# A two-layer hybrid backbone: the input projection by seven products instead of eight, and its outputs through DRAM

## The chip, the cores and the metric

The kernel runs on one core of one Trainium2 chip. A core has TensorE (PE in the profile) for matmuls, VectorE (DVE), ScalarE (ACT) and GpSimd (POOL) for elementwise work, and SyncE (SP), which here only starts transfers. Each engine works through its own instructions in their order and waits for the others by semaphores. Times are microseconds of one execution on the device; the time of a kernel is the median of its runs.

## The reference, cut to what matters

Two layers over 1024 tokens of a sample and 128 tokens of a prompt, width 1024. The prompt is computed with the same weights, without the cached keys. For each layer:

```
hn   = rms_norm(x, g_pre) * (1 + scale) + shift        # scale, shift, gate from w_mod
proj = hn @ w_in                                       # 1024 x 7456
a_b, a_c, a_x, a_z, q_down, kv_down, b_z, c_u, c_z, merge_logits = split(proj)
y_a  = silu(a_z) * (a_b * conv3(a_c * a_x))
y_b  = silu(b_z) * attention(rms_norm(q_down) @ w_uq, [cache, rms_norm(kv_down) ...] @ w_ukv)
y_c  = silu(c_z) * (pool(c_u) @ pool_w) * pool_scale   # window means of 2, 4, 8, 16 tokens
merged = sum(sigmoid(merge_logits) * (y_n @ w_branch[n]) for n in a, b, c)
x    = x + gate * rms_norm(merged @ w_o, g_post)
```

## The kernel before, in words

All large products are float32 products made of three: each operand is split in a high part that TensorE's float32r format holds, and a low part with the rest. `mm3` (line 107) issues high x high, high x low and low x high by `mm` (line 105), each 128x128 weights against up to 512 columns. A split takes a cast (`a_copy`, ACT, or `p_copy`, POOL) for the high part and a subtraction on DVE (`sub`, line 88) for the low one.

The sample's tokens are held with features on the partitions, in two chunks of 512 tokens. `hn` of a chunk is 8 contraction blocks, split (`hn_tile`). w_in comes in 15 groups of 512 columns (the last 256), in weight tiles of 128x1024 that SP loads, POOL or ACT casts and DVE completes (`pump`). There are 44 slots of 128x1040 (`S`), 12 of 128x512 (`H`) and 8 accumulators of 128x512 (`PS`). `in_group` (line 471) multiplies a group: four blocks of 128 columns for chunk 0 (`prod_m`), the prompt with its tokens on the partitions (`prod_p`, 24 matmuls of 512 columns), then chunk 1 (`prod_k`).

A layer is: `conv_phase` (groups 0 to 3, the convolution after each), `merge_phase` of branch 0 (groups 4 and 5 are its gates, w_branch follows each), `pool_phase` (groups 6 to 8), `merge_phase` of branch 2 (groups 9, 10), `kvq_phase` (groups 11 to 14: latents, queries, gates of the attention branch), `produce` (queries, keys, values), `attention`, `last_merge` and `out_phase` (w_o and the norms after it). What follows an output of w_in (convolution, window sums, norms, the prompt's parts) reads it from the accumulator or from SBUF and is written out in the stretches in which the next groups are multiplied: work is kept in generators, and each `tick()` between two blocks moves the oldest ones on by one step (`spawn`, `tick`, `finish`, lines 115 to 135). So the order in each engine's queue is that in which this code calls; there is no scheduler. Only the merge's sums (`d_part`), the attention's gates and silu(b_z) go through DRAM.

In `merge_phase` an old sum is fetched one block ahead, and a store follows the product:

```
def out(c, m, gate, ps, g=g):
    mul(gate, ps, gate)
    if not first:
        add(gate, gate, old.pop((c, m)), eng=pool)
    sp.dma_start(out=d_part[4 * g + m, c], in_=gate)
```

## Time and profile before

| | |
|---|---|
| median of 3 runs | 2762.57 us (2761.93 to 2763.33) |
| span of the profiled execution | 2761.7 us, first to last instruction; 0.9 us under the median |
| PE busy | 2670.2 us (97%), 11696 matmuls recorded |
| DVE busy | 1262.9 us (46%) |
| ACT busy | 871.4 us (32%) |
| POOL busy | 677.7 us (25%) |
| mean granted clock of PE | 0.990 |
| read from HBM, written | 167.16 MB, 43.81 MB |

Busy time is the time in which an engine works on an instruction; an engine that waits in an instruction is idle. The mean of a matmul's duration (395 ns) is longer than the distance from one to the next, since they are pipelined; their rate is read from a stretch with a count. A group of instructions says how long its engine was idle right before them, and whom it waited for. The chain of waits follows the last instruction back to what released it, step by step.

### The profile page before, as it was taken

The numbers are of one execution on the slowest core, as the hardware profiler recorded it, in microseconds if no ns is written. First come the engines' busy times: TensorE is split into PE (matmuls) and PEld (weight loads), VectorE is DVE, ScalarE is ACT, GpSimd is POOL, SyncE is SP. The second block draws the span as 40 slices with busy tenths as digits, with TensorE's granted clock in tenths as the row PEclk, the third lists the DMA queues.
The fourth block names the chain that finished last, engine by engine and source line by source line (L and its number), as shares of the span: only waits on it lengthen the run. The fifth ranks groups of instructions, "written<-read, shape, count | busy, mean of one in ns | idle before, by whom it ended". The sixth has DMA issues, their size and how long they took to land.

```text
span 2761.7 us, 29939 instructions
## 1 busy us (share of the span) xinstructions
PE 2670.2 (97%) x11696; PEld 2114.9 (77%) x11696; DVE 1262.9 (46%) x1802; ACT 871.4 (32%) x1547; POOL 677.7 (25%) x598
## 2 busy tenths in 40 slices
PE   6999999999999999999989999999999999999998
PEld 3787777788888777777768888888888787777786
DVE  5532212521243378886475321134113416888655
ACT  3211111221123367773332111122102324777622
POOL 3200000001210355662132000100121023576502
PEclk8999999999999999999999999999999999999999
DMA  6111433223312100006231102202232120000333
GB/s 262 46 38 54 165 121 115 80 84 107 117 45 102 58 5 9 24 31 206 80 118 46 46 23 73 100 23 85 95 103 85 54 95 20 5 8 31 122 119 115
DMA packets 83149, 215.08 MB, mean 78 GB/s; under 512 B 10304, under 2 KB 12608, under 8 KB 83008
## 3 DMA queue, kind: packets, MB, share of 16 engines
q1 hardware_dynamic: 74656, 199.01, 21.1%
q10 hardware_dynamic: 8352, 14.16, 1.4%
q8 instruction: 92, 1.51, 0.2%
q14 instruction: 49, 0.40, 0.0%
HBM read 167.16 MB, written 43.81 MB: 76 GB/s over the span
## 4 chain that ended last, share of the span: by engine, by line
PE 85%; DVE 7%; issue 3%; ACT 3%; POOL 1%; DMA 0%; SPq 0%; DVEq 0%; ACTq 0%; POOLq 0%
PE p L105 85%; DVE s L86 4%; DVE c L1163 1%; ACT s L77 1%; ACT h L77 1%; ACT s L66 1%; POOL s L101 1%; DVE h L86 0%; DVE c L1170 0%; POOL s L86 0%; DVE s L98 0%; DMA s<-in_xT_dram 0%; DVE h L98 0%; DVE h L101 0%; ACT h L1081 0%
## 5 line engine op out<-in xcount | busy, mean ns | idle before, releaser
L105 PE MATMUL p<-s,s 128*128 128x512 f32 (+3 forms) x10948 | 2582.7, 395 | 35.0 <-DVE c L1163 13.0
L105 PEld LDWEIGHTS p<-s,s 128*128 128x128 f32 (+1 forms) x10948 | 2030.5, 188 | 551.4 <-issue 30.9
L77 ACT ACTIVATE h<-p 128x512 f32<-128x512 f32 (+1 forms) x496 | 288.3, 584 | 744.6 <-PE p L105 727.3
L86 DVE TENSOR_TENSOR s<-s,s 128x1024 fp32r<-128x1024 f32 (+5 forms) x263 | 303.2, 1163 | 422.5 <-ACT s L66 206.5
L80 POOL TENSOR_SCALAR s<-s 128x1024 fp32r<-128x1024 f32 (+2 forms) x144 | 172.5, 1201 | 1303.3 <-PE p L105 598.2
L86 DVE TENSOR_TENSOR s<-h,s 128x512 fp32r<-128x512 f32 (+3 forms) x348 | 316.7, 921 | 159.6 <-ACT s L66 90.6
L86 DVE TENSOR_TENSOR h<-p,h 128x512 f32<-128x512 f32 (+4 forms) x166 | 100.0, 609 | 317.2 <-PE p L105 278.0
L77 ACT ACTIVATE s<-p 128x512 fp32r<-128x512 f32 (+1 forms) x320 | 193.9, 606 | 105.4 <-PE p L105 101.1
L66 ACT CAST s<-s 128x1024 fp32r<-128x1024 f32 (+3 forms) x96 | 96.5, 1007 | 220.3 <-DVE s L86 122.5
L86 POOL TENSOR_TENSOR h<-h,h 128x512 f32<-128x512 f32 (+2 forms) x76 | 91.3, 1201 | 276.2 <-DVE h L86 240.7
L1163 DVE TENSOR_REDUCE c<-p 128x1 f32<-128x448 f32 x256 | 147.8, 611 | 4.3 <-PE p L105 4.1
L66 ACT CAST s<-h 128x512 fp32r<-128x512 f32 (+4 forms) x124 | 66.8, 542 | 249.5 <-DVE h L86 95.8
L86 DVE TENSOR_TENSOR h<-h,h 128x512 f32<-128x512 f32 (+8 forms) x118 | 73.9, 627 | 154.9 <-ACT h L77 149.7
L86 POOL TENSOR_TENSOR s<-s,s 64x1024 fp32r<-64x1024 f32 (+3 forms) x43 | 102.9, 2393 | 81.3 <-DVE s L86 55.2
L66 ACT COPY s<-p 64x512 f32<-64x512 f32 (+3 forms) x136 | 76.5, 568 | 129.5 <-PE p L105 125.5
L86 POOL TENSOR_TENSOR s<-h,s 128x512 fp32r<-128x512 f32 x64 | 89.2, 1393 | 113.3 <-ACT s L77 110.8
L66 ACT COPY h<-p 128x512 f32<-128x512 f32 (+3 forms) x74 | 34.1, 464 | 254.2 <-PE p L105 157.6
L86 POOL TENSOR_TENSOR s<-s,h 128x512 f32<-128x512 f32 x38 | 57.1, 1513 | 151.2 <-DVE h L98 106.7
L86 DVE TENSOR_TENSOR s<-p,s 128x512 fp32r<-128x512 f32 (+2 forms) x62 | 36.2, 586 | 93.1 <-PE p L105 75.9
L86 POOL TENSOR_TENSOR h<-h,s 128x512 f32<-128x512 f32 x32 | 51.9, 1624 | 9.0 <-DMA h<-d_bz 7.7
L77 ACT ACTIVATE h<-h 128x512 f32<-128x512 f32 (+1 forms) x50 | 31.4, 628 | 44.7 <-DVE h L101 34.7
L86 DVE TENSOR_TENSOR c<-p,vec 128x4 f32<-128x4 f32 x24 | 3.8, 157 | 87.2 <-PE p L105 87.1
(115 smaller groups left out, 845.4 us busy)
## 6 DMA issues: line engine op xcount, KB each, us to landing
s<-in_w_in_dram SPq DMA_DIRECT2D x116, 512.0 KB
s<-in_w_mod_dram SPq DMA_DIRECT2D x48, 512.0 KB
d_part<-h SPq DMA_DIRECT2D x64, 256.0 KB
h<-d_part SPq DMA_DIRECT2D x64, 256.0 KB
s<-in_w_br_dram SPq DMA_DIRECT2D x24, 512.0 KB
s<-in_xT_dram SPq DMA_DIRECT2D x16, 512.0 KB
d_gate<-h ACTq DMA_DIRECT2D x32, 256.0 KB
s<-in_w_o_dram SPq DMA_DIRECT2D x16, 512.0 KB
```

The costliest lines, as they stand in the source:

```text
L66: act.copy(out=out, in_=in_)
L77: act.activation(out=out, in_=in_, func=func, scale=scale, bias=bias)
L80: pool.tensor_scalar(out=out, in0=in_, scalar1=1.0, scalar2=0.0, op0=ALU.mult, op1=ALU.add)
L86: eng.tensor_tensor(out=out, in0=in0, in1=in1, op=op)
L101: (eng or dve).tensor_scalar(out=out, in0=in0, scalar1=s1, scalar2=s2, op0=op0, op1=op1)
L105: pe.matmul(out=out, lhsT=lhsT, rhs=rhs, start=start, stop=stop)
L1163: dve.reduce_max(out=mv[:, i, qt:qt + 1], in_=ps[:, 0:448], axis=AX.X)
```

## The change

The products of hn with w_in for the two chunks are computed by Strassen's scheme in the form with seven products. The contraction is cut in two halves, the tokens in two chunks and the columns in two blocks of 128, so a unit (`Pair`) is 256 columns of w_in; a layer has 29. Of hn there are seven sets, each of four contraction blocks and 512 tokens, split in two: 11, 21 and 22 (halves of hn itself) and T1 to T4 (sums of them, from `t_gen`); they hold 28 of the 44 slots. Of the weights there are the two halves and two sums. Six pairs of each layer are done in two steps (`early`: the two products that chunk 0 alone needs, and the prompt; later the other five). The prompt's products are now pieces of 256 columns.

All 29 pairs come first (`in_phase`). Their outputs (gates after the sigmoid, a_c * a_x, a_b * silu(a_z), c_u, silu(c_z), latents and so on) are stored in DRAM. The convolution of the sample runs from DRAM to DRAM beside the later pairs (`conv_gen`). Then `mid_phase` loads the convolution's results and runs the two merges with the pooling, the prompt's convolution and pooling, the norms of latents and queries as generators beside them; `produce` and the rest follow as before. The pieces of w_mod in the background are now fetched one at a time, one tick ahead (`mod_bg`).

The diff, cut to its core:

```diff
     def mod_bg(todo):
         for l, j in todo:
-            for i in range(2):
-                sts = [S(), S()]
-                for n, st in enumerate(sts):
-                    sp.dma_start(out=st[:, 0:1024], in_=I["w_mod"][l, j, 2 * i + n])
-                yield
+            for i in range(4):
+                st = S()
+                sp.dma_start(out=st[:, 0:1024], in_=I["w_mod"][l, j, i])
                 yield
...
+    def hn_f32(l, c, kp, x, r, on_pool=False):
...
+        for j in range(2):
+            k, o = 2 * kp + j, slice(512 * j, 512 * j + 512)
+            stt(x[:, o], x[:, o], A_(l, 1, k), r, ALU.mult, ALU.mult)
...
+    def t_gen():
+        def put(name, j, x):
+            hi, lo = S(F32R), S(F32R)
+            a_copy(hi[:, n], x[:, n])
+            sub(lo[:, n], x[:, n], f(hi[:, n]))
+            X[name][j] = (hi, lo)
...
+        for j in range(2):
+            sub(t1[j][:, n], b12[j][:, n], b11[j][:, n])
+            sub(t2[j][:, n], b22[j][:, n], t1[j][:, n])
+        for j in range(2):
+            sub(b21[j][:, n], b21[j][:, n], t2[j][:, n], eng=pool)
+        for j in range(2):
+            put("T2", j, t2[j])
+        yield
...
+    class Pair:
+        def prep(self):
+            raw = [S(), S()]
...
+                for t in range(2):
+                    src = I["w_in"][self.l, g, 2 * i + t].rearrange("p (k c)->p k c", k=2)
+                    sp.dma_start(out=raw[i][:, 512 * t:512 * t + 512].rearrange("p (k c)->p k c", k=2),
+                                 in_=src[:, :, 256 * h:256 * h + 256])
+            yield
...
+                s = [S(), S()]
+                add(part(s[0], 0), part(raw[0], 1), part(raw[1], 1), eng=pool)
+                sub(part(s[0], 1), part(raw[0], 0), part(raw[0], 1), eng=pool)
+                yield
+                sub(part(s[1], 0), part(s[0], 0), part(raw[0], 0))
+                sub(part(s[1], 1), part(raw[1], 0), part(s[1], 0))
+                yield
...
+        def prod(self, w, half, name):
+            ps = PS()
+            for i in range(4):
+                o, q = 256 * i + 128 * half, slice(512 * (i % 2), 512 * (i % 2) + 512)
+                hi, lo = X[name][i // 2]
+                mm3(ps, (w[0][:, o:o + 128], w[1][:, o:o + 128]), (hi[:, q], lo[:, q]), i == 0, i == 3)
+            return ps
...
+    def early(l, units, epis, mid, pend):
+        for b in range(0, NE, 3):
+            us = units[b:b + 3]
+            for u in us:
+                ready(u)
...
+            for u in us:
+                h = H()
+                a_copy(h, u.prod(u.w[0], 0, "11"))
...
+            for u, h in zip(us, p1):
+                v = H()
+                add(v, u.prod(u.w[1], 0, "21"), h)
...
+            finish(*pend)
+            for u in us:
+                epis[u.p][1](u.prompt())
...
+    def run(l, u, epi):
+        ready(u)
+        full = u.kind == "full"
+        p = H()
+        if full:
+            a_copy(p, u.prod(u.w[0], 0, "11"))
+            ahead(u, 1)
+            v = H()
+            add(v, u.prod(u.w[1], 0, "21"), p)
+            epi[0](0, 0, v)
+            ahead(u, 1)
+            epi[1](u.prompt())
+        else:
+            sp.dma_start(out=p, in_=d_p1[u.p])
+        ahead(u, 1)
         tick()
...
+        add(p, u.prod(u.s[1], 0, "T2"), p)
+        ahead(u, 1)
+        p5 = u.prod(u.s[0], 0, "T1")
+        v = H()
+        add(v, p5, p)
...
+    def merge(l, n, y, yp, first, pend):
...
+            nxt = fetch(0, 0)
             for m in range(4):
+                cur = nxt
+                nxt = fetch(0, m + 1) if m < 3 else fetch(1, 0)
+                out(0, m, prod_m(B, m, y_get(y), 0), cur)
                 tick()
...
+    def s_pool(l, gis, yc):
+        for gi in gis:
+            u, z = S(), S()
...
+            for c in range(2):
+                sp.dma_start(out=u[:, 8 + 512 * c:520 + 512 * c], in_=d_u[gi, c])
+                sp.dma_start(out=z[:, 512 * c:512 * c + 512], in_=d_z[gi, c])
+            yield
+            o = pooled(u, gi, 1024, [S(), S()])
...
+    def mid_phase(l):
+        yp = S(F32R)
+        gc = spawn(p_conv(l, yp))
+        ya = load_ya(l)
+        lead[0] = 4
+        fill()
+        yc, ypc = {}, S(F32R)
+        gp = [spawn(p_pool(l, ypc)), spawn(s_pool(l, range(4), yc))]
+        merge(l, 0, ya, yp, True, (gc,))
+        finish(*gp)
+        rel()
+        R = kvq_post(l)
+        for g in R["gens"]:
+            spawn(g)
         lead[0] = 5
+        merge(l, 2, yc, ypc, False, ())
         finish(*R["gens"])
...
         for l in range(L):
-            ya, yp, gens = conv_phase(l, pend, None if l else mid())
-            if l == 0:
-                spawn(gmod)
-            merge_phase(l, 0, 4, ya, yp, gens, True)
-            yc, yp, gens = pool_phase(l)
-            merge_phase(l, 2, 9, yc, yp, gens, False)
-            R = kvq_phase(l)
+            in_phase(l, units, None if l else mid(), pend)
+            R = mid_phase(l)
             A = produce(l, R)
```

The first place where the order is told is DVE's queue at the window sums of the pooling in layer 0. In the listings, a name is a buffer with its numbers (s a slot, h a half, p an accumulator), an `x2` at a row's end a count. Before, the window sums of two groups of c_u (`s382`, `s384`, in SBUF since their eviction) follow the rows of a w_mod piece, beside the next group of w_in:

```order
L86 TENSOR_TENSOR h438_2999<-p435_2991,h438_2999 128x512
L86 TENSOR_TENSOR h438_2999<-h438_2999,h439_3000 128x512
L86 TENSOR_TENSOR s442_3010<-s382_2593 128x1039
L98 SCALAR_TENSOR_TENSOR s443_3011<-s442_3010,s382_2593 128x1024
L86 TENSOR_TENSOR s443_3011<-s442_3010,invc_83 128x1
L86 TENSOR_TENSOR s443_3011<-s443_3011,s382_2593 128x1
L86 TENSOR_TENSOR s445_3017<-s443_3011,s444_3016 128x1024
L86 TENSOR_TENSOR s446_3020<-s384_2597 128x1039
L86 TENSOR_TENSOR s447_3021<-s446_3020 128x1037
```

In the changed kernel the first group (`s989`, loaded from `d_u`) stands behind the prompt's pooling (`h1003` to `h1006`), and behind it come the evictions of the first merge (`p1012`, `p1014`) and the low part of pool_w (`s1018`):

```order
L88 TENSOR_TENSOR h1004_5810<-h1004_5810,h1003_5809 128x1
L88 TENSOR_TENSOR h1006_5819<-h1004_5810,h1006_5819 128x128
L88 TENSOR_TENSOR s1007_5835<-s989_5734 128x1039
L100 SCALAR_TENSOR_TENSOR s1008_5836<-s1007_5835,s989_5734 128x1024
L88 TENSOR_TENSOR s1008_5836<-s1007_5835,invc_93 128x1
L88 TENSOR_TENSOR s1008_5836<-s1008_5836,s989_5734 128x1
L88 TENSOR_TENSOR s1010_5842<-s1008_5836,s1009_5841 128x1024
L88 TENSOR_TENSOR h991_5742<-p1012_5847,h991_5742 128x512
L88 TENSOR_TENSOR h1011_5845<-p1014_5864,h1011_5845 128x512
L88 TENSOR_TENSOR s1018_5883<-s980_5704,s1017_5882 128x512
```

The window sums moved from the stretch of a w_in group to that of the first merge's products, with the low part of the weight that the next small products read behind them.

The second place is DVE's queue in the first microseconds of layer 0 with all of x. Before, the norm of the second chunk (`s27` to `s30`) gave high and low parts at once, beside evictions and weights of the first two groups:

```order
L98 SCALAR_TENSOR_TENSOR s27_149<-s27_149,cols0_1_88,h101_469 128x512 x2
L98 SCALAR_TENSOR_TENSOR s104_491<-s27_149,cols0_1_88,s103_490 128x512 x2
L86 TENSOR_TENSOR s106_499<-s28_150,s105_498 128x512 x2
L86 TENSOR_TENSOR s60_265<-p76_348,s60_265 128x512
L98 SCALAR_TENSOR_TENSOR s29_151<-s29_151,cols0_1_88,h101_469 128x512 x2
L98 SCALAR_TENSOR_TENSOR s108_522<-s29_151,cols0_1_88,s107_521 128x512 x2
L86 TENSOR_TENSOR s110_530<-s30_152,s109_529 128x512 x2
L86 TENSOR_TENSOR h113_565<-p111_539,h112_564 128x128 x2
L86 TENSOR_TENSOR s120_601<-s73_342,s119_600 128x1024
```

In the changed kernel the norm (`s29` to `s32`) is followed by the sums T1 and T2 (`s128` to `s131`), then by the low parts of T2, T1, T3, 22 and T4, and these by the low part of pair 5's second weight (`s155`). From the first low part on:

```order
L88 TENSOR_TENSOR s133_586<-s130_577,s132_585 128x1024
L88 TENSOR_TENSOR s135_590<-s131_578,s134_589 128x1024
L88 TENSOR_TENSOR s137_596<-s128_575,s136_595 128x1024
L88 TENSOR_TENSOR s139_600<-s129_576,s138_599 128x1024
L88 TENSOR_TENSOR s141_604<-s29_169,s140_603 128x1024
L88 TENSOR_TENSOR s143_608<-s30_170,s142_607 128x1024
L88 TENSOR_TENSOR s145_612<-s31_171,s144_611 128x1024
L88 TENSOR_TENSOR s147_616<-s32_172,s146_615 128x1024
L88 TENSOR_TENSOR s149_620<-s4_108,s148_619 128x1024
L88 TENSOR_TENSOR s151_624<-s5_109,s150_623 128x1024
L88 TENSOR_TENSOR s155_656<-s123_533,s154_655 128x1024
```

On PE the last of these rows is read by the product of pair 5 with set 21, whose first rows are:

```order
L107 MATMUL p179_818<-s96_426,s154_655 128x512
L107 MATMUL p179_818<-s96_426,s155_656 128x512
L107 MATMUL p179_818<-s97_427,s154_655 128x512
L107 MATMUL p179_818<-s96_426,s154_655 128x512
L107 MATMUL p179_818<-s96_426,s155_656 128x512
```

Before, twelve rows of 512 columns of the norm stood in front of the next weight's low part (`s120`); now eight of them do, and fourteen of 1024 columns for the sums and splits.

## Rows read from the trace of the kernel before

**Rows 1.** The page: busy time by engine, then shares of the chain.

```profile
PE 2670.2 (97%) x11696; PEld 2114.9 (77%) x11696; DVE 1262.9 (46%) x1802; ACT 871.4 (32%) x1547; POOL 677.7 (25%) x598
...
PE 85%; DVE 7%; issue 3%; ACT 3%; POOL 1%; DMA 0%; SPq 0%; DVEq 0%; ACTq 0%; POOLq 0%
```

**Rows 2.** Windows by stage: each engine's busy us and instructions, then clock, DMA.

```profile
core 0: us, PE busy (x) PEld busy (x) DVE busy (x) ACT busy (x) POOL busy (x), PEclk, DMA share, GB/s
66.70:960.00 893.30, 892.27 (x3957) 708.26 (x3956) 278.26 (x427) 166.91 (x286) 107.99 (x108) 1.00 0.26 88
960.00:1060.00 100.00, 91.50 (x414) 70.69 (x413) 79.41 (x138) 60.75 (x124) 46.38 (x50) 0.98 0.01 4
1060.00:1290.00 230.00, 218.42 (x959) 169.85 (x958) 182.88 (x240) 158.63 (x289) 145.30 (x104) 0.99 0.18 59
...
1440.00:2300.00 860.00, 860.00 (x3746) 696.52 (x3745) 264.21 (x374) 162.56 (x271) 107.49 (x108) 1.00 0.20 68
```

**Rows 3.** Timeline of PE in layer 0: start, duration, matmuls.

```profile
142.18 50.07 PE L105 MATMUL p<-s,s 128*128 128x512 f32 x216
```

**Rows 4.** Groups by form, PE: count | busy, mean ns | idle before.

```profile
L105 PE MATMUL p<-s,s 128*128 128x512 f32 x10242 | 2495.3, 397 | 17.4 <-ACT s L77 7.0 <-DVE s L86 4.1 <-ACT h L1081 2.0
```

**Rows 5.** A window around the 24 matmuls of 256 columns of layer 0.

```profile
906.61:909.45 2.84, 2.84 (x25) 2.84 (x24) 0.00 (x0) 0.60 (x1) 1.88 (x2) 1.00 0.94 330
```

**Rows 6.** Groups by form, DVE, the whole span.

```profile
L86 DVE TENSOR_TENSOR s<-s,s 128x1024 fp32r<-128x1024 f32 x178 | 224.3, 1275 | 354.9 <-ACT s L66 179.8 <-PE p L105 86.7 <-POOL s L80 81.5
...
L86 DVE TENSOR_TENSOR h<-p,h 128x512 f32<-128x512 f32 x112 | 76.5, 688 | 277.3 <-PE p L105 270.4 <-DMA h<-in_bmod_g_dram 4.1 <-DMA h<-d_part 2.1
L86 DVE TENSOR_TENSOR h<-h,h 128x512 f32<-128x512 f32 x92 | 68.0, 740 | 151.5 <-ACT h L77 149.7 <-DMA h<-in_gpost_r_dram 0.3
...
L98 DVE SCALAR_TENSOR_TENSOR h<-p,vec,s 128x512 f32<-128x512 f32 x16 | 11.9, 747 | 22.3 <-PE p L105 22.3
L98 DVE SCALAR_TENSOR_TENSOR s<-s,cols,h 128x512 f32<-128x512 f32 x12 | 11.9, 1033 | 0.0
```

**Rows 7.** Groups by form, ACT, the whole span.

```profile
L77 ACT ACTIVATE h<-p 128x512 f32<-128x512 f32 x462 | 279.0, 604 | 722.5 <-PE p L105 710.6 <-DVE s L86 6.5 <-ACT h L77 2.7
...
L66 ACT CAST s<-s 128x1024 fp32r<-128x1024 f32 x70 | 73.1, 1048 | 194.0 <-DVE s L86 122.5 <-PE p L105 32.1 <-DMA s<-in_w_in_dram 31.3
L66 ACT CAST s<-h 128x512 fp32r<-128x512 f32 x82 | 50.9, 621 | 150.6 <-DVE h L86 71.6 <-DVE h L98 44.8 <-POOL h L86 20.0
...
L66 ACT COPY h<-p 128x512 f32<-128x512 f32 x44 | 25.7, 585 | 129.9 <-PE p L105 94.4 <-PE p L714 21.3 <-issue 14.2
```

**Rows 8.** Groups by form, POOL, the whole span.

```profile
L80 POOL TENSOR_SCALAR s<-s 128x1024 fp32r<-128x1024 f32 x124 | 150.1, 1212 | 1190.0 <-PE p L105 534.5 <-DVE s L86 352.8 <-DMA s<-in_w_in_dram 191.3
...
L86 POOL TENSOR_TENSOR h<-h,h 128x512 f32<-128x512 f32 x52 | 70.1, 1348 | 227.0 <-DVE h L86 191.7 <-issue 24.8 <-DMA h<-d_part 10.2
```

**Rows 9.** Groups by form, DVE, 66.7 to 960 us.

```profile
L86 DVE TENSOR_TENSOR s<-s 128x1039 f32<-128x1039 f32 x4 | 4.9, 1234 | 0.0
...
L86 DVE TENSOR_TENSOR h<-h 128x143 f32<-128x143 f32 x4 | 1.2, 298 | 0.0
...
L86 DVE TENSOR_TENSOR c<-c 128x1 f32<-128x1 f32 x6 | 1.0, 159 | 1.6 <-ACT c L77 1.5
```

**Rows 10.** Timeline of DVE at a norm of layer 0 and its splits.

```profile
761.27 0.69 DVE L101 TENSOR_SCALAR h<-p 128x512 f32<-128x512 f32 x1
763.37 0.97 DVE L86 TENSOR_TENSOR h<-h,h 128x512 f32<-128x512 f32 x1 [1.41 <-ACT h L77]
...
767.27 0.69 DVE L86 TENSOR_TENSOR s<-h,s 128x512 fp32r<-128x512 f32 x1 [0.69 <-ACT s L66]
```

**Rows 11.** Windows before and at the end of layer 0.

```profile
1290.00:1375.00 85.00, 85.00 (x366) 68.63 (x365) 46.34 (x57) 25.64 (x41) 10.46 (x6) 1.00 0.28 99
1375.00:1440.00 65.00, 53.56 (x205) 41.69 (x204) 49.67 (x59) 22.73 (x39) 25.41 (x26) 0.89 0.44 157
```

More of the change, by code (lines that the diff above doesn't have):

```diff
@@ new lines, in keep_prod, with epi, epip @@
+    def keep_prod(dst, dstp, func):
+        got = {}
+        def epi(j, c, x):
+            if j == 0 and func:
+                a_fn(x, x, func)
+            if c not in got:
+                got[c] = x
+                return
+            y = got.pop(c)
+            mul(x, x, y, eng=pool)
+            sp.dma_start(out=dst[c], in_=x)
+        def epip(ps):
+            h = H()
+            if func:
+                a_fn(h[:, 0:128], ps[:, 0:128], func)
+            else:
+                a_copy(h[:, 0:128], ps[:, 0:128])
+            mul(h[:, 128:256], ps[:, 128:256], h[:, 0:128])
+            sp.dma_start(out=dstp, in_=h[:, 128:256])
+        return epi, epip
@@ new lines, in hybrid_step_kernel, with units_of, in_phase @@
+    SOURCE = [(g, h) for g in (4, 5, 9, 10, 0, 1, 2, 3) for h in range(2)]
+    SOURCE += [(11, 0), (11, 1), (12, 0)] + [(g, h) for g in (6, 7, 8) for h in range(2)]
+    SOURCE += [(12, 1), (13, 0), (13, 1), (14, 0)]
+    ORDER = list(range(8, 23)) + [6, 7] + list(range(23, 29))
+    def units_of(l):
+        e = [Pair(l, p, "early") for p in range(NE)]
+        preps.extend(e)
+        return e
+    def in_phase(l, e, mid, pend):
+        epis = pairs(l)
+        u = [Pair(l, p, "late") for p in range(NE)] + [Pair(l, p, "full") for p in ORDER]
+        preps.extend(u)
+        early(l, e, epis, mid, pend)
+        if l == 0:
+            spawn(gmod)
+        finish(*[g for g in pend])
+        convs = None
+        for x in u:
+            if x is u[-1]:
+                lead[0] = 2
+                wlim[0] = wend[l]
+            run(l, x, epis[x.p])
+            if x.p == 17:
+                convs = spawn(conv_gen(l))
+        finish(convs)
@@ L745, in kvq_phase, with kvq_post @@
+    def kvq_post(l):
+        R = {"ckv": [(S(F32R), S(F32R)) for _ in range(2)], "pp": S(F32R), "qn": {}}
         pp = R["pp"][:, 0:1024].rearrange("p (h k t)->p h k t", h=2, k=2)
@@ new lines, in norm @@
+        def norm(c, blocks, n, gain, outs):
+            o = 512 * c
+            xs = [H() for _ in blocks]
+            for x, b in zip(xs, blocks):
+                sp.dma_start(out=x, in_=d_kvq[b, c])
+            yield
+            acc = H()
+            a_fn(acc, xs[0], AF.Square)
+            for x in xs[1:]:
+                q = H()
+                a_fn(q, x, AF.Square)
+                add(acc, acc, q)
+            yield
+            r = rstd(bsum(acc), n)
+            for k, x in enumerate(xs):
+                stt(x, x, v_(l, gain, k), r, ALU.mult, ALU.mult)
+                hi, lo = outs[k]
+                split(hi[:, o:o + 512], lo[:, o:o + 512], x)
+            yield
@@ L835, in p_kv, with latents @@
+        def latents():
+            for c in range(2):
+                yield from norm(c, (0, 1), 256, V_GKV, R["ckv"])
+                yield from rope(c)
+            for k in range(3):
+                R["qn"][k] = (S(F32R), S(F32R))
+            for c in range(2):
+                yield from norm(c, (3, 4, 5), 384, V_GQ, R["qn"])
+        def p_kv():
             e, eq = H(), H()
-            R["pe"] = eq
-            a_copy(e[:, 0:384], ps[:, 0:384])
-            a_copy(eq[:, 0:128], ps[:, 384:512])
+            sp.dma_start(out=e[:, 0:384], in_=d_kvqp[:, 0:384])
+            sp.dma_start(out=eq[:, 0:384], in_=d_kvqp[:, 384:768])
+            yield
@@ L1368, in out_group @@
                 pump(pumps[m])
+            if pre:
+                ahead(None, 2)
+                ahead(None, 2)
             tick()
@@ L1418, in post_chunk @@
         for i, kp in enumerate((0, 1, 2, 3)):
-            hn_tile(l + 1, c, kp, O_[kp], r2, kp % 2)
+            hn_f32(l + 1, c, kp, O_[kp], r2, kp % 2)
             if i == 1:
                 yield
+        if c:
+            yield
+            yield from t_gen()
     def out_prompt(l, xp, gps, out, cs):
```

679 lines of the change are left out of this document (334 added, 345 removed).

## The prediction

> **What bounds the kernel now.** I read four views in this order: the page's busy shares and chain, the busy time by stage, the timeline of TensorE (PE), then the groups by form. PE is busy for 97% of a span of 2761.7 us, and 85% of the chain that ended last is its matmuls [rows 1]. By stage the reader is to see where the rest goes [rows 2]. In the long stretch of layer 0 in which all of w_in and two of the three merges run (66.7 to 960 us), PE loses 1.03 of 893.3 us, and the stretch of layer 1 from 1440 to 2300 us loses nothing; VectorE (DVE) is busy there for 31%. So convolution, pooling, norms and merges cost PE nothing in the kernel before: they lie beside w_in's matmuls. Where DVE is busy for 79% or 80% (attention and what leads to it), PE loses 8.5 of 100 us and 11.6 of 230. The matmuls go at a steady rate: 216 of 512 columns in 50.07 us, 0.2318 us each [rows 3].
>
> **What PE saves.** Of w_in for the two chunks, a layer has 58 blocks x 2 chunks x 8 contraction blocks x 3 = 2784 matmuls; seven products of 12 for 29 pairs are 2436. Two layers save 696. The prompt's products go from 512 to 256 columns: 14 groups x 24 x 2 = 672 matmuls of 512 leave, 1344 of 256 come. The trace has 10242 matmuls of 512 columns [rows 4], so 1368 fewer is 13%. At 0.2318 that is -317.1 us. For 256 columns the last group of a layer has 24 in a row: 2.84 us, 0.1183 each [rows 5], so +159.0. The sum is -158.1 us of PE. Were the pieces of 256 free of any extra it would be -158.5, so this term is safe to a few us.
>
> **What w_in's pairs cost the others.** A full pair is 84 matmuls of 512 and 24 of 256: 22.3 us of PE. Beside it DVE has seven additions from PSUM (0.688), two strided sums (not shown before; 0.69 to 0.75 by the rows of 512), four low parts of 1024 (1.275): 11.4 us [rows 6]. ScalarE (ACT) has three casts of 1024 (1.048), a copy (0.585) and up to four activations of about 0.6: 6.6 us; GpSimd (POOL) one cast (1.212) and two sums (1.35): 3.9 [rows 7, 8]. So DVE is at 51% and PE stays the bound here; The sample's convolution, 16 instructions of 1024 columns (some 20 us by the same rows), runs beside the later pairs and fits too. A full pair moves 1 MB of weights in and up to 1 MB of outputs out: some 94 GB/s, near the 88 and 68 of these stretches before [rows 2], and far under the 330 of [rows 5]. I price the 46 full pairs' stalls at 0, with PE as the cover, and keep a rival for it.
>
> **The stage between w_in and the attention.** Here the cover goes. In the kernel before the pooling's window sums stand among evictions of w_in; now `mid_phase` runs after the last w_in product, with only the branch products for PE. PE's listing from there to the first matmul that waits for the last query norm has 496 matmuls of 512 columns (115.0 us) and 34 small ones (some 3): 118 us. DVE's queue from w_in's last eviction to that norm has 251 instructions:
> - 19 with two inputs of 1024 at 1.275: 24.2; 14 of the window sums and means at 1.23: 17.2
> - 74 of 512 with two inputs at 0.69: 51.1; 26 scalar_tensor_tensor at 0.747: 19.4; 18 others over 512 columns at 0.69: 12.4
> - 52 of 128 to 143 columns at 0.31: 16.1; 10 of 256 to 768 at some 0.5: 5.2; 38 of a few columns at 0.16: 6.1
>
> Together 152 us [rows 6, 9], against PE's 118, where the stretch before had 278 against 892. DVE also stands idle in its own chains. A norm's two ACT steps cost it 1.41 us and each cast of 512 between product and low part 0.69 [rows 10]; with 4 norms, 18 casts of 512, 4 of 1024 (about 1.1, from ACT's 1.048) and some 5 us for the narrow ones it is 27 us. PE's own small products between two DVE steps (eight for the pool weights, six sets of transposes, four sums) add three matmuls each, 0.7 x 18 = 12. DVE's time is then 191 and PE loses 73. The loads of u, z, gates and old parts now stand on SP's queue behind stores that wait for DVE or POOL: behind the first store stand the loads for PE's transposes and for the window sums, and in DVE's queue the low part of pool_w stands behind the window sums, so PE's first pool product is late by all of these. Before, POOL waited for d_part in all 10.2 us [rows 8], 5 a layer: taken once more, 78 us per layer. The bounds: 34 (DVE's busy time alone, all hops hidden) and 112 (some 30 such loads, each behind a store, with one hop of 1.3 us each on top of 73). 78 lies near the sum of rows, and I take it. Two layers: +156.
>
> **The starts of the two layers.** In layer 0 the second chunk's norm and `t_gen`'s splits stand in one piece in DVE's queue in front of the low part of pair 5's second weight. From the norm's first row to that one it is 8 scalar_tensor_tensor (1.033 [rows 6]) and 15 of 1024: 27.4 us and the casts between them. PE has 72 matmuls of 256 and 60 of 512 until it needs it: 22.4 us. DVE comes late there too (it has the first splits behind it): 5 to 15, I take 10. The first late pair's weights and the first piece of w_mod wait on SP for slots that these splits free: 3 to 13, I take 7. Less cover for the first chunk's last norm: 3. Layer 1 does its norm and sums beside w_o, where DVE was at 76% and PE lost 11.4 of 65 us already [rows 11], and then the early pairs: 5 to 10, I take 8. Together +28, from 13 to 41.
>
> **PE's clock.** In that same stretch the granted clock averaged 0.89: of its two levels PE had 1.2 GHz for a part, after waits of a few us. Its 205 matmuls were busy for 53.56 us, where the stretch ahead took 85.0 for 366, or 47.6 for as many: 6 us [rows 11]. I add 5 per layer (0 to 20): +10. The Trainium skill ("TensorE: Matmul & The Clock Gate", section "HAM oscillation — how this bites in real kernels") says that short bursts of matmuls between waits fall back to the low clock each time, so that the cost is paid again and again. The trace agrees for these rows, and the new stage has PE in just such bursts; what it would make of the time is the rival of PE's clock.
>
> **Sum.** -158 + 156 + 28 + 10 = +36 on 2761.7, so 2798; the timed median, 2762.57, is 0.9 above the profiled span, so 2799 us.
>
> **The rivals.**
> - Faster: the order of the new stage overlaps as attention does. For it: with DVE at 80%, PE lost only 5% there [rows 2]. Against: in the new stage DVE has more than PE, not less. With both layers' stages at 34 and the starts at 13 it is 2762.6 - 158 + 68 + 13 = 2686. From a stage stall of about 57 us a layer downward the kernel is faster, with the other terms as I have them.
> - Slower by PE's clock: every burst of the new stage at 1.2 GHz. PE's 118 us become 236, more than DVE's 196 with its waits, and the stage takes 40 us more in place of the 5: 2799 + 70 = 2869. For it: the 0.89 of [rows 11]. Against: bursts there are 12 matmuls and more, and the stages of [rows 2] with losses still had 0.98.
> - Slower by w_in itself: 28 of 44 slots are held by the seven sets of sums, so the next pair's weights come late, and each of 46 full pairs loses 2 us: +92, 2891. For it: POOL waited 191.3 us for w_in loads before [rows 8]. Against: PE lost nothing through that, and the slack of a pair is 22.3 - 11.4.
>
> **How the numbers follow.** A change of 0.2% (5.5 us) is about what can be told from none. My forecast has 0.45 (its own range 2768 to 2865), the faster rival 0.33 (2686 to 2757), the clock 0.08, w_in 0.07; 0.07 is left for the terms cancelling to within 0.2%. Faster is 0.33, same 0.07, slower 0.45 + 0.08 + 0.07 = 0.60. The ends of all terms are -158 + 68 + 13 = -77 (2686) and -158 + 224 + 41 + 40 = +147 (2910). The range for 8 of 10 cuts the lower tail hardly and the upper more: 2690 to 2880.
>
> **What would show it.** In the new trace 24 matmuls of 256 take 2.8 us, a full pair 22 to 23 us with PE at its rate, and PE's busy sum is lower by about 160. Between w_in and the attention a stretch of some 200 us a layer has PE at 60% and DVE at 75% or more, with PE waiting for DVE's low parts, and DVE for ACT. If PE loses under 57 us in each such stretch, the sign is wrong, by the step that I trust least: how much of the 152 + 27 + 12 runs one behind the other. If pairs take 24 us or more, w_in is bound by something that I counted as hidden. If PE's clock in that stretch is below 0.8, the clock was mis-sized.

## The result

The changed kernel takes 3057.97 us (median of 4 runs, 3055.58 to 3062.53), where the kernel before took 2762.76: 1.107 times as long (95% interval 1.1053 to 1.1085). The forecast was slower, 2799 us, with 2690 to 2880 as its range; the direction is right and the size is not. The span of the profiled execution is 3060.7 us, 299.0 more than before.

The page of the changed kernel gives busy time by engine, to be read against [rows 1]:

```profile
PE 2625.0 (86%) x11672; PEld 2065.9 (67%) x11672; DVE 1827.8 (60%) x2440; ACT 1028.6 (34%) x1710; POOL 868.7 (28%) x727
```

PE is busy for 45 us less and yet the kernel is 299 us longer: PE now stands idle for 436 us and not for 91. By stage (one window each: length, then busy us of PE, PE's weight loads, DVE, ACT and POOL, then PE's clock, DMA share, GB/s), to be read against [rows 2]:

```profile
67.00:141.40 74.40, 48.72 (x266) 40.74 (x265) 51.72 (x51) 30.59 (x40) 23.69 (x11) 0.84 0.20 65
141.40:411.30 269.90, 237.22 (x1017) 164.64 (x1017) 111.49 (x160) 48.57 (x68) 51.38 (x40) 0.92 0.44 144
411.30:833.60 422.30, 418.15 (x2006) 347.27 (x2004) 233.26 (x265) 102.82 (x140) 78.04 (x61) 1.00 0.35 114
833.60:1079.50 245.90, 143.47 (x515) 107.25 (x516) 138.55 (x235) 45.15 (x77) 34.79 (x42) 0.77 0.47 156
1586.00:1700.00 114.00, 72.39 (x329) 57.61 (x330) 75.87 (x75) 44.06 (x60) 35.51 (x26) 0.78 0.31 105
...
2313.00:2555.00 242.00, 139.39 (x514) 104.80 (x514) 136.48 (x233) 42.69 (x75) 34.62 (x42) 0.77 0.47 155
```

The reader is to see three kinds of stretch. From 411 to 834 us, and nearly so in layer 1 from 1700 to 2313, the pairs run at PE's rate. From 834 to 1079.5 and from 2313 to 2555 the stage between w_in and the attention has PE at 58% and DVE at 56% (143.47 and 138.55 of 245.90 us): no engine is busy for most of it. And the layers' starts (67 to 141, 1586 to 1700) and the pairs beside which w_mod is fetched (141 to 411) lose too. PE's waits over the whole span follow (us in total, times, the longest). In the rows of the changed kernel L107 is `mm`, L68 a cast or copy by ACT, L79 an ACT function, L82 a cast by POOL, L88 a sum, difference or product of two operands:

```profile
PE p L107 <- ACT s L68: 131.6, 27, 23.1
PE p L107 <- DVE h L88: 120.7, 12, 27.3
PE p L107 <- DVE s L88: 41.8, 29, 9.1
PE p L107 <- DMA s<-in_w_mod_dram: 28.0, 8, 7.7
...
PE p L1045 <- DVE h L103: 23.3, 2, 11.8
PE p L107 <- DMA h<-in_perm_dram: 12.6, 2, 6.8
```

For an account I take each recorded matmul at its full rate, 0.2318 us for 512 columns and in proportion for others (the 96 of two columns at some 0.06), and call the rest of a stretch its loss. Waits and a slow clock are both in it.

| stretch | PE's work | loss | loss before, same work |
|---|---|---|---|
| to 67 us | 29.5 | 37.8 | 31.6 |
| early pairs of layer 0, to 141 | 44.3 | 29.8 | 3.1 |
| pairs beside w_mod, to 411 | 210.6 | 59.3 | none |
| other pairs of layer 0, to 834 | 414.5 | 7.8 | none |
| stage of layer 0, to 1079.5 | 113.5 | 132.4 | none |
| queries, keys, attention, to 1416 | 284.1 | 52.4 | 32.8 |
| w_o and early pairs of layer 1, to 1700 | 214.9 | 69.1 | 19.9 |
| pairs of layer 1, to 2313 | 592.7 | 20.3 | 3.9 |
| stage of layer 1, to 2555 | 113.3 | 128.7 | none |
| queries, keys, attention, to 2900 | 298.7 | 46.3 | 34.2 |
| the end | 146.5 | 14.2 | 13.6 |

The sums are 2463 and 598 after, 2624 and 138 before: 161 us of work saved, 460 us of loss added.

### The profile page after: what moved, and what is told of

Its sections match the earlier page's. It is cut to its first block, busy times and chain, and to the rows that moved or that the text cites. A ratio compares the mean times of both kernels' runs of the same rounds, so it can differ in the third digit from the quotient of the medians.

```text
span 3060.7 us, 32318 instructions
## 1 busy us (share of the span) xinstructions
PE 2625.0 (86%) x11672; PEld 2065.9 (67%) x11672; DVE 1827.8 (60%) x2440; ACT 1028.6 (34%) x1710; POOL 868.7 (28%) x727
## 3 DMA queue, kind: packets, MB, share of 16 engines
q1 hardware_dynamic: 175136, 291.05, 29.2%
## 5 line engine op out<-in xcount | busy, mean ns | idle before, releaser
L107 PE MATMUL p<-s,s 128*128 128x512 f32 (+3 forms) x10924 | 2498.9, 388 | 188.2 <-ACT s L68 124.2
L107 PEld LDWEIGHTS p<-s,s 128*128 128x128 f32 (+1 forms) x10924 | 1975.3, 192 | 694.4 <-ACT s L68 131.5
L88 DVE TENSOR_TENSOR s<-s,s 128x1024 fp32r<-128x1024 f32 (+4 forms) x519 | 627.1, 1217 | 308.5 <-ACT s L68 146.9
L88 DVE TENSOR_TENSOR h<-p,h 128x512 f32<-128x512 f32 (+3 forms) x556 | 368.4, 665 | 506.0 <-PE p L107 373.3
L88 DVE TENSOR_TENSOR s<-h,s 128x512 fp32r<-128x512 f32 (+5 forms) x356 | 325.8, 926 | 154.2 <-ACT s L68 87.9
L88 POOL TENSOR_TENSOR s<-s,s 128x512 f32<-128x512 f32 (+2 forms) x109 | 203.1, 1865 | 736.6 <-DMA s<-in_w_in_dram 543.4
L68 ACT CAST s<-s 128x1024 fp32r<-128x1024 f32 (+1 forms) x255 | 257.0, 1023 | 345.1 <-DVE s L88 184.4
L79 ACT ACTIVATE h<-h 128x512 f32<-128x512 f32 (+1 forms) x216 | 135.6, 628 | 643.3 <-DVE h L88 527.5
L82 POOL TENSOR_SCALAR s<-s 128x1024 fp32r<-128x1024 f32 (+2 forms) x125 | 155.8, 1249 | 652.1 <-DVE s L88 244.0
L79 ACT ACTIVATE h<-p 128x512 f32<-128x512 f32 (+2 forms) x364 | 208.7, 573 | 250.8 <-PE p L107 236.3
L88 POOL TENSOR_TENSOR h<-h,h 128x512 f32<-128x512 f32 (+2 forms) x108 | 141.0, 1307 | 308.7 <-DVE h L88 173.1
L79 ACT ACTIVATE s<-p 128x512 fp32r<-128x512 f32 x288 | 174.1, 604 | 2.4 <-POOL h L88 2.4
L88 DVE TENSOR_TENSOR h<-h,h 128x512 f32<-128x512 f32 (+6 forms) x134 | 87.5, 653 | 128.3 <-ACT h L79 111.8
L68 ACT COPY h<-p 128x512 f32<-128x512 f32 (+1 forms) x112 | 53.6, 483 | 317.2 <-PE p L107 286.3
L68 ACT CAST s<-h 128x512 fp32r<-128x512 f32 (+4 forms) x132 | 71.7, 546 | 262.1 <-DVE h L100 86.0
L107 PE MATMUL p<-h,ones 128*128 128x512 f32 x32 | 28.0, 972 | 120.8 <-DVE h L88 120.7
L88 POOL TENSOR_TENSOR s<-h,s 128x512 fp32r<-128x512 f32 x64 | 88.8, 1387 | 123.7 <-ACT s L79 122.3
L107 PEld LDWEIGHTS p<-h,ones 128*128 128x128 f32 x32 | 7.1, 270 | 126.0 <-DVE h L88 118.4
L68 ACT COPY s<-p 64x512 f32<-64x512 f32 (+3 forms) x112 | 62.2, 565 | 83.7 <-PE p L107 58.9
L88 POOL TENSOR_TENSOR s<-s 128x512 f32<-128x512 f32 x58 | 76.0, 1311 | 0.0
L88 POOL TENSOR_TENSOR s<-s,h 128x512 f32<-128x512 f32 x26 | 40.2, 1552 | 116.1 <-DVE h L100 114.3
```

The source lines that it names most:

```text
L68: act.copy(out=out, in_=in_)
L79: act.activation(out=out, in_=in_, func=func, scale=scale, bias=bias)
L82: pool.tensor_scalar(out=out, in0=in_, scalar1=1.0, scalar2=0.0, op0=ALU.mult, op1=ALU.add)
L88: eng.tensor_tensor(out=out, in0=in0, in1=in1, op=op)
L107: pe.matmul(out=out, lhsT=lhsT, rhs=rhs, start=start, stop=stop)
```

## The experiments

All but e9 are parts of one plan: undo one suspected cost at a time in the changed kernel, then all together, then the same orders with eight products. Times are of one or two runs, beside a kernel before of 2762 to 2768 us.

**e1: the splits in front of a weight.** In the changed kernel PE waits twice for the place that the second order excerpt showed (timeline of PE: start, length, matmuls, the wait in front in brackets):

```profile
118.51 0.80 PE L107 MATMUL p<-s,s 128*128 128x512 f32 x1 [21.55 <-ACT s L68]
```

The same view in layer 1:

```profile
1678.28 0.79 PE L107 MATMUL p<-s,s 128*128 128x512 f32 x1 [23.08 <-ACT s L68]
```

```diff
-            finish(*pend)
+            finish(*pend[:1])
             for u in us:
                 epis[u.p][1](u.prompt())
```

> Edit: in the early pairs only the prompt's norm is finished before the prompt's products; the second chunk's norm and the seven sets' splits go on step by step at the ticks. Theory (order in DVE's and ACT's queues: the splits stand in one piece ahead of pair 5's weight): the waits of 21.6 and 23.1 us in front of pair 5's product in the two layers fall to under 6 each, the whole by 30 to 45 us. Rival (the work is too much whatever its order): the wait comes back at the first product with a sum T, a few us later, and the whole gains 10 us or less.

3039.3 us, some 19 less. PE's largest waits from 60 to 160 us:

```profile
PE p L107 <- ACT s L68: 13.0, 1, 13.0
PE p L107 <- ACT s L79: 9.9, 1, 9.9
PE p L107 <- DMA s<-in_w_mod_dram: 7.9, 1, 7.9
```

The wait of 21.6 us is one of 13.0, now at the first product with a sum T; 23.1 became 12.7 in layer 1. The 19 us lie between the two forecasts, so each theory has half: the order was worth some 10 us a layer, and the wait came back at the first sum T, as the rival said. What is left is, I take it, the amount of work that ACT and DVE have to do before the late pairs can begin.

**e2: w_mod fetched earlier.**

```diff
                 sp.dma_start(out=st[:, 0:1024], in_=I["w_mod"][l, j, i])
                 yield
+                yield
```

> Edit: a piece of w_mod is fetched two ticks ahead and not one. Theory (one tick of about 6 us is too short for a 512 KB load that takes 5.5 us and stands behind stores): the 28.0 us in which PE waits for w_mod (8 times) fall to under 6, the clock between 141 and 411 us rises from about 0.93 to 0.97, the whole falls by 25 to 40 us. Rival (that stretch loses by weights that come late, since each piece takes one of the 44 slots): holding a piece for longer makes the weights later, and the whole is the same or slower by up to 15 us.

3030.6 us, 27 less. The window from 141 to 411 us has PE at 0.98 of its clock and 96% busy, where the changed kernel had 0.92 and 88%:

```profile
141.00:411.00 270.00, 260.07 (x1181) 195.14 (x1180) 137.15 (x179) 56.69 (x80) 64.69 (x50) 0.98 0.41 136
```

The theory holds, though PE still waits 6.7 us for w_mod in this window (10.7 in the whole kernel) where under 6 was expected. The kernel before fetched a piece two steps ahead; the change made it one, in steps of some 6.7 us.

**e3 and e10: stores off SP's queue.** SP's own queue in the changed kernel's stage of layer 0 (line 854 stores d_part, 873 the prompt's part, 843 loads a gate):

```profile
SPq L854 <- DVE h L88: 63.1, 11, 17.5
SPq L854 <- POOL h L88: 28.7, 9, 10.1
SPq L873 <- DVE h L88: 22.8, 2, 11.7
SPq L843 <- DVE h L88: 21.0, 3, 9.3
```

```diff
-                sp.dma_start(out=d_part[4 * g + m, c], in_=gt)
+                pool.dma_start(out=d_part[4 * g + m, c], in_=gt)
...
-            sp.dma_start(out=d_partp[g], in_=gp)
+            pool.dma_start(out=d_partp[g], in_=gp)
```

e3 has the first of the two edits, e10 both.

> Edit: in the two merges the stores of d_part are issued by POOL and no longer by SP, so that loads on SP don't stand behind a store that waits. Theory A (SP's queue: SP waits 63 us for DVE and 39 us for POOL in front of these stores, in one layer's stage): the stage between w_in and the attention falls from 246 to 190 to 215 us, the whole by 60 to 110 us. Rival B (DVE's own work and chains, 152 us and 44 us of hops): under 20 us in all. Rival C (the 12 half slots: the loads wait for slots, not for their turn): under 30 us in all.

2980.2 us, 78 less. The stage of layer 0 falls from 246 to 213.5 us, and DVE's waits in it for gates (d_gate) from 19.1 to 4.3:

```profile
DVE s L88 <- ACT s L68: 26.1, 34, 2.2
DVE h L88 <- ACT h L79: 13.9, 9, 2.6
DVE h L88 <- PE p L107: 7.0, 5, 2.2
...
DVE h L88 <- DMA h<-d_gate: 4.3, 2, 3.9
```

Theory A is right for 33 us a layer, and for the 12.6 us in which PE waited for the perm table at the head of the attention's part. It is not all: 100 us of the stage's loss stay. The waiting store has not vanished either, it now holds POOL's queue. In the stage of layer 1, POOL stands in front of two of these stores, and a cast that PE reads stands behind them (timeline of POOL in e3):

```profile
2300.20 1.13 POOL L854 DMA_DIRECT2D d_part<-h  x2 [17.72 <-DVE h L88]
```

PE's waits for POOL's casts over the whole span grow by it from 4.3 to 18.8 us, 14.5 of them in one piece.

> Edit: as e3, and the stores of the prompt's part (d_partp) by POOL too. In e3 SP still waited 39.4 us in a layer's stage in front of these two stores, 27.6 in one piece. Theory A (a store that waits on SP holds the loads behind it): the stage falls from 213.5 to 190 to 205 us, the whole from 2980 by 15 to 45. Theory B (what is left is DVE's work with its hops): under 8 us in all.

2967.2 us, 13 less, and the stage at 208 us: both a little short of what theory A asked for. In the queue the waits of 39.4 us for the prompt's stores are gone, and SP waits longer for half slots that a store holds (34.0 us, 20.5 in e3):

```profile
SPq L843 <- DMA d_part<-h: 34.0, 9, 10.0
SPq L843 <- DVE h L88: 28.4, 4, 12.2
```

**e4: other slots for the merge.**

```diff
-                gt, old = H(), None
+                gt, old = S()[:, 0:512], None
...
-                    old = H()
+                    old = S()[:, 0:512]
```

> Edit: the gates and old sums of the merges are loaded to full slots (44, of which most are free in this stage) and not to the 12 half slots. Rival C (half slots): the norms' loads come early, the PE waits of 13.8 and 26.9 us in front of the sums of squares fall to under 8 each, the stage from 246 to under 205 us, the whole by over 80 us. Theory A (SP's queue) and rival B (DVE): the loads still stand behind the stores, or DVE has no time for them; under 30 us in all.

3051.7 us: 6 less, within what a single run can tell. The waits of 13.8 and 26.9 us stood at 14.2 and 25.2. In the order of the changed kernel the half slots were not what held the loads back.

**e5 and e6: parts of the stage back beside w_in.** e5 is e3 with the window sums beside the last pairs, from DRAM to DRAM; e6 adds the norms.

```diff
+    def pool_gen(l):
+        for gi in range(4):
...
+            yield
+            o = pooled(u, gi, 1024, [S(), S()])
+            yield
+            sp.dma_start(out=d_o[gi], in_=o[:, 0:1024])
...
+    def norm_gen(l):
...
+                    x = H()
+                    sp.dma_start(out=x, in_=d_kvq[b, c])
+                    yield
+                    if acc is None:
+                        acc = H()
+                        a_fn(acc, x, AF.Square)
+                    else:
+                        a_fn(x, x, AF.Square)
+                        add(acc, acc, x)
+                yield
+                r = rstd(bsum(acc), n)
```

> Edit: as e3 (stores of d_part by POOL), and the sample's window sums and means of the pooling are worked out beside the last eight pairs of w_in, from DRAM to DRAM, as the convolution is; the merge's stage only loads, splits and multiplies them. Theory B (what is left of the stage's loss, about 100 us a layer in e3, is DVE's work in one chain with PE): 17 us of DVE's work, 4 us of hops and the loads of c_u leave, so the stage falls from 213 by 15 to 35 us in each layer, the whole by 30 to 70 against e3's 2980. Rival A (loads behind others on SP): the number of loads stays nearly the same; under 15 us in all. If the pairs are not a cover, the pairs' stretch grows by as much as the stage falls.

2959.9 us, 20 less than e3. The stage ends 196 us after w_in, 17 earlier than in e3, and DVE's busy time in it falls by 19, from 138 to 119. The pairs give part of it back: the same matmuls take 8 us longer in each layer. For the stage theory B holds, at the low end; the 20 us of the whole lie between rival A (under 15) and theory B (30 to 70).

> Edit: as e5, and the norms of the latents and queries (loads, squares, sums over partitions, 1/sqrt, scaling) beside w_in's pairs too, back to DRAM; the stage only loads and splits them. Theory (the waits in front of the four sums of squares, 9 + 19 + 5 us in layer 0 of e3, are a chain of load, square, sum and low part that nothing covers): a further 30 to 45 us per layer leave, 50 to 90 in all against e5. Rival (DVE's queue as a whole, whatever stands in it: 4 norms are 4 x 4.5 us of its work): about 20 per layer. Rival (half slots: 12 tiles for both pairs and norms): the pairs slow by as much as is won.

2967.3 us, 7 more than e5. The window of the pairs, then of the stage:

```profile
410.00:879.00 469.00, 431.46 (x2004) 352.93 (x2002) 275.35 (x319) 121.98 (x164) 80.74 (x69) 0.96 0.38 128
879.00:1037.00 158.00, 128.28 (x526) 100.99 (x526) 96.05 (x172) 31.41 (x57) 49.98 (x62) 0.90 0.67 233
```

The stage is 158 us, 38 less, as the theory said. But what stands ahead of it and behind it loses at least as much: the same matmuls take 34 and 30 us longer in the pairs of the two layers and 12 and 17 in the queries and the attention, whose part was not looked into. In the pairs of layer 0 PE waits 22.3 us for DVE in front of the four sums over partitions: load, square and add did not fit in one step between two products.

**e7, e11: all together.** e7 is e1, e2 and e6 with the prompt's convolution beside the pairs; e11 adds the second store of e10 and two steps in `norm_gen` (one more `yield` behind the load, one in front of `bsum`).

> Edit: e1, e2, e3, e5 and e6 together, and the prompt's convolution beside the pairs as well. If the losses are separate they add: about -20 (e1), -30 (e2), -80 (e3), -50 (e5), -70 (e6), -10 for the prompt's convolution, so 2800 +- 30. If they hide one another (a wait that goes shows the next one behind it), 2850 to 2900. Under 2762, the kernel before, only if the starts of the layers gain more than e1 has shown.

2933.4 us (1.061 times before, 1.0583 to 1.0645), over both forecasts. The first of them added up guesses: e5 and e6 had been put at 120 us, and their runs gave 13. The gains that the runs did measure (19 for e1, 27 for e2, 78 for e3, 20 for e5, 7 lost in e6) sum to 137 us, and e7 has 125 of them: they nearly add.

> Edit: as e7, with the prompt's stores as in e10, and in the norms beside the pairs one more step between a load and its square and between the last sum and PE's sum over partitions. Theory (in e7 PE waited 5 to 8 us in front of each such sum because one step of about 6 us is shorter than load, square and add): these waits go, the pairs' stretch of layer 0 loses under 40 us instead of 64, and the whole falls from 2933 to 2850 to 2900. Rival (the half slots or DVE's order hold the pairs up): under 20 us.

2893.8 us (1.046, 1.0418 to 1.0503), 40 less, as the theory said for the whole. Where it came from was not as expected: in the pairs of layer 0 the same matmuls take only 11 us less, and their loss is 57 us, not under 40; 8 and 12 us went from the queries and the attention of the two layers. The waits for sums (19.0 us in e7) are gone from the pairs; those for the casts and low parts of weights are not (18.2 and 4.8 in e7). PE's waits from 490 to 841 us:

```profile
PE p L107 <- ACT s L68: 19.4, 7, 9.7
PE p L107 <- DVE s L88: 10.3, 9, 4.7
PE p L107 <- ACT h L68: 1.8, 1, 1.8
```

The window of the stage:

```profile
841.00:990.00 149.00, 126.28 (x520) 99.92 (x521) 92.60 (x156) 32.53 (x53) 52.03 (x67) 0.92 0.76 255
```

The stage is 149 us now and DVE is busy for 93 of them. The fastest version found is still 127 us over the kernel before (2767.1 us, run beside it).

**e8, e12: the same orders with eight products.** Each block of 128 columns is summed over eight contraction blocks in one accumulator; no sums of weights, tokens or products. Four sets of hn are held. One thing more differs: the early pairs now do all of chunk 0 (48 matmuls of a pair and not 24, besides the prompt), so PE has more to do before it needs the second chunk.

```diff
-        for n in ("11", "21", "22", "T1", "T2", "T3", "T4"):
+        for n in ("11", "21", "12", "22"):
...
+        def both(self, half, c, ps=None, ks=(0, 1)):
+            ps = ps or PS()
+            for k in ks:
+                for i in range(4):
...
+                    mm3(ps, (w[0][:, o:o + 128], w[1][:, o:o + 128]), (hi[:, q], lo[:, q]), k == i == 0, k == 1 and i == 3)
+            return ps
```

> Edit: the changed kernel's order with eight products instead of seven: w_in first, outputs through DRAM, the stage, the prompt in pieces of 256, but no sums of weights or tokens and no sums of products; each block is accumulated over all eight contraction blocks. It tells the order's cost from the scheme's gain. PE's work is then 2624 us again. Theory (the loss is the order's: stage, prompt and starts): the stage stays at 240 to 250 us per layer, the waits at the layers' starts shrink (two sets fewer to split before), the whole is 3060 + 161 - 40 to - 80, so 3140 to 3180. Rival (the scheme's own DVE and ACT work makes the loss): the pairs and starts lose less by over 100 us, and the whole is under 3100.

3126.4 us, a little under what the theory gave. The early pairs lose nothing and the stage is as long as with seven:

```profile
67.00:141.00 74.00, 74.00 (x395) 63.09 (x394) 30.52 (x36) 38.31 (x54) 6.62 (x4) 1.00 0.39 130
...
880.30:1125.30 245.00, 141.81 (x518) 106.13 (x519) 137.61 (x235) 45.33 (x78) 32.68 (x42) 0.77 0.45 152
```

This splits the result. The order alone (w_in first, outputs through DRAM, the stage behind it), as written here with w_mod one step ahead and the stores on SP, costs 364 us against the kernel before. The seven products, in that order, give back 68 of the 161 us that they save on PE.

> Edit: the order of e11 (everything mended) with the eight products of e8. It tells what the seven products are worth once the stage is shorter. Theory (the seven products give back most of their 161 us of PE in the pairs and the starts, because their sums and splits hold DVE, ACT and the slots): the waits at the starts and inside the pairs, about 100 us in e11, are mostly gone; the whole is 2880 to 2930, within 40 us of e11's 2894. Rival (the scheme keeps in this order what e8 showed, 66 us, or more as the cover grows): 2960 to 3050.

2897.0 us (1.048, 1.0446 to 1.0515), 3 from e11, which the runs can't tell from nothing. PE is busy for 386.1 of 387.5 us in the later pairs with eight products, convolution, pooling and norms beside them:

```profile
67.00:450.00 383.00, 382.52 (x1824) 301.54 (x1822) 72.49 (x91) 110.57 (x162) 25.27 (x20) 1.00 0.34 112
450.00:837.50 387.50, 386.11 (x1828) 309.46 (x1828) 100.57 (x141) 117.83 (x180) 2.66 (x10) 1.00 0.46 155
837.50:992.00 154.50, 130.42 (x537) 103.07 (x536) 90.48 (x157) 33.55 (x55) 54.46 (x70) 0.93 0.74 253
```

By the same account e12 loses 267 us on 2624 of work and e11 426 on 2463. In the mended order the seven products are worth nothing: what PE saves it waits. Two rows of PE's waits over the whole span, casts and low parts, have most of the difference. In e11:

```profile
PE p L107 <- ACT s L68: 103.7, 26, 12.4
PE p L107 <- DVE s L88: 48.7, 41, 6.7
```

In e12 they are 25.2 and 20.2. Whether the splits come late by the work of the sums or by the 28 slots that the seven sets hold was not separated. Nor was the seven-product scheme tried in the order of the kernel before, so what it is worth with that cover stays open.

**e9: is it PE's clock?** The stage's granted clock was 0.77, and over the whole kernel PE's busy time is 162 us over its full rate, 46 before. e9 fills two waits with matmuls that nobody reads.

```diff
+        def fill_pe(n):
+            if n:
+                ps, w = PS(), yc[0][0]
+                for i in range(n):
+                    mm(ps, w[:, 0:128], w[:, 0:512], i == 0, i == n - 1)
```

> Edit, on the changed kernel: in front of the second and third sum of squares of the stage, where PE waits 13.8 and 26.9 us, 48 and 96 matmuls of 512 columns (11.1 and 22.3 us at the full rate) whose result nobody reads. Theory (a part of the loss is PE's clock, which falls to 1.2 GHz in the waits; busy time over the full rate grew from 46 to 162 us): the waits shrink by the length of the filler, the 48 to 60 matmuls behind each run at 0.232 and not at 0.27 to 0.29, the granted clock of the stage rises from 0.77 to 0.88 or more, and the whole falls by 4 to 15 us though 288 matmuls were added. Rival (the slow matmuls are slow by their own waits, not by the clock): same rate behind the filler, the whole is the same or longer by up to 20 us.

3052.8 us. The windows of the first filler, the rest of the wait, and the 48 matmuls behind it:

```profile
986.83:997.90 11.07, 11.06 (x49) 8.82 (x47) 7.46 (x9) 1.05 (x1) 6.06 (x5) 1.00 0.58 189
997.90:1001.56 3.66, 0.70 (x3) 0.37 (x3) 2.44 (x6) 1.56 (x3) 0.00 (x0) 0.96 0.00 0
1001.56:1014.54 12.98, 12.98 (x51) 10.12 (x49) 6.77 (x10) 2.50 (x4) 2.53 (x2) 0.88 0.18 60
```

The window of the whole stage:

```profile
835.60:1082.00 246.40, 179.50 (x674) 137.04 (x675) 138.96 (x235) 44.56 (x77) 36.39 (x44) 0.83 0.46 154
```

The same work in the changed kernel, the stage and then the 48 matmuls:

```profile
836.58:1084.00 247.42, 147.97 (x528) 110.82 (x529) 138.72 (x235) 44.29 (x77) 37.26 (x44) 0.77 0.47 153
1003.77:1017.30 13.53, 13.52 (x50) 10.22 (x48) 6.77 (x10) 2.50 (x4) 2.55 (x2) 0.85 0.20 59
```

The filler ran at the full clock (1.00). A wait of 3 us was left behind it, and the 48 matmuls after that had 0.88, hardly more than without a filler (0.85); the 60 behind the second filler took 15.77 us and not 16.12. So this run does not show the rate that the theory asked for, and the stage's 0.83 is the filler's own: PE's time over its full rate fell only from 31.5 to 29.2 us. What it shows is that the waits in front of the sums have room: the stage, 246.4 us with 144 matmuls and 32 us of PE's time more, is as long as without them (247.4). What a full clock for the matmuls that count would be worth stays open. By way of DVE there is little room for it: DVE waits for PE for 11 us in the whole stage of the changed kernel. Whether the clock costs something at the starts was not tried.

## Why the prediction was wrong

- **What PE saves** was right: the pairs run as worked out, 647 matmuls, six pairs but one matmul, in 133.7 us, 22.3 each. Against the -158 of the forecast the account has -161, which is no other measurement: it counts a piece of 256 as half of 512 columns, and 696 matmuls at 0.2318 are 161.3. (The -158.5 in the forecast for this case is a slip for -161.3. Two more sums are off without effect: ACT's part of a pair is 6.1 us by its terms, not 6.6, and the lower end of the starts 16, not 13.) The 0 us for the pairs' stalls was 26 for both layers (28.1 less 3.9 in the table, and 1.4 by which a stretch that it calls none was under its count before), most of it in the pairs beside the convolution.
- **The stage** was right in kind and place and 105 us short: 261 us and not 156 (132.4 and 128.7 a layer, where I gave 112 as the upper bound). DVE's part can be read term by term. In the stage of layer 0 it is busy for 138.6 us (forecast 152) and idle for 107. DVE's waits there, in us:

```profile
DVE s L88 <- ACT s L68: 28.4, 35, 3.2
DVE h L88 <- DMA h<-d_gate: 19.1, 8, 4.8
DVE h L88 <- ACT h L79: 14.0, 10, 2.9
DVE h L88 <- PE p L107: 8.2, 4, 3.0
DVE h L88 <- DMA h<-d_gatep: 6.0, 1, 6.0
DVE s L88 <- POOL s L82: 4.9, 2, 2.6
DVE h L88 <- DMA h<-in_cosT_dram: 4.9, 1, 4.9
```

For ACT it is 49 in all (forecast 27), for PE 11 (12), for loads 33 (5), for POOL 8 (0), with lesser rows. The step that failed is "taken once more, 78 us per layer": I saw the loads behind stores on SP's queue and priced them by the 10 us that POOL had waited for d_part before. e3 measured it: 33 us a layer. With it failed the 27 us for ACT's hops, 22 too low: the rows have 35 waits for casts (28.4) and 10 for functions (14.0), where I counted 22 casts, 4 norms and 5 us for narrow ones. My upper bound added 39 for the loads to a sum that this left too low. So DVE was busy for 56% of the stage, not for 75% or more.
- **The starts** were right in place and mis-sized: 82 us and not 28. The wait that I put at 10 us was 21.6 + 1.5, and layer 1, which I priced at 8, has the same wait of 23.1 and two more, 7.5 in front of a norm's sum over partitions and 8.7 in front of a cast behind it; the kernel before had 2.8, 3.7 and 4.9 in that place.
- **w_mod** was missed: the pairs beside it lose 59 us. I had its first piece in a term of 7 and no term for the others. The diff showed it: one piece and one step ahead where two steps stood. A step there takes some 6.7 us (270 us for 32 pieces and 8 ends of a group). The group of the loads in these pairs (count, size, median us from issue to landing) and SP's two largest waits in front of them show why one step is short:

```profile
s<-in_w_mod_dram SPq DMA_DIRECT2D x32, 512.0 KB, 3.7
```

The waits of SP's queue in the same window:

```profile
SPq L316 <- PE p L107: 42.8, 10, 11.6
...
SPq L316 <- DMA d_gate<-h: 17.0, 5, 5.8
```

The transfer takes half a step, and the issues themselves wait on SP for 84 us (2.6 each, in these and three lesser rows), besides what stands ahead of them. PE's waits for w_mod are 28 of the 59 us, 5 are others, and the remaining 27 are matmuls in a stretch whose clock averaged 0.92. With one step more (e2) the waits for w_mod are 6.7, the clock is 0.98 and the same window loses 23 us and not 59; some 8 come back in the pairs behind it, which leaves the 27 of the whole. The 23 are 10 of waits and 13 of matmuls over their full rate.
- **The clock** I added as +10 and had as a rival. The clock did fall (0.926 against 0.990 over the whole). PE's busy time over its full rate grew by 116 us: 56 of them lie in the two stages, and the other 60 in the losses of the starts, the pairs and the attention. The rival (every burst of the stage at 1.2 GHz) did not come: long waits there had a granted clock of 0.57 and 0.68, the 48 and 60 matmuls behind them 0.85 and 0.89. Still, 0.77 is under the 0.8 that the forecast had named as the sign of a mis-sized clock. The rule of the Trainium skill that I cited ("TensorE: Matmul & The Clock Gate", section "HAM oscillation — how this bites in real kernels") says that bursts between waits fall back each time, and the rows agree, 0.77 in the stage. What that cost is not shown, since e9 left the rate of these matmuls nearly as it was.
- **The attention** was not in the forecast: 32 us more loss in both layers together. 12.6 of it are waits for a table whose load stands behind the stores (gone in e3); the rest is not settled.

The terms with the wrong size: stage +105, w_mod +59, starts +54, attention +32, pairs +26, PE -3, less the 10 for the clock: 263 of the 263 us between 2798 and 3061.

## What to carry to other kernels

Before a scheme that saves matmuls is priced, ask what the matmuls cover: here each layer's w_in products hid convolution, pooling, norms and merges at no cost, and putting them in a row cost 364 us as first written, and 133 in the best order found (e12), where the scheme could save 161 and in that order saved nothing. In a stage without cover, add up the in-order chain of the engine that sits between the others, every hop to a neighbour and every load with what stands ahead of it on its queue; do not price it by busy shares, since in the stage no engine was over 60%. A store that waits should not stand in front of loads: moving it from SP's queue to POOL's gave 78 us here. But look at what then stands behind it, since in e3 a cast on POOL came late by it and PE waited 14.5 us.

## What was not expected of the hardware

Filling 22 and 11 us of a wait with matmuls held PE at its full clock during the filler, but 3 us of idling behind it were followed by a stretch at 0.88 all the same (e9). And the traffic of the late pairs did not hold them up: the 272 loads of w_in in 256 KB pieces took 4.3 us to land (median), and the late pairs of e12 moved 155 GB/s with PE busy for 99.6%.
